# Loading the adaLN slabs from GpSimd's queue instead of SyncE's in a hybrid decoder layer

## The chip, the core and the metric

The kernel runs on one core of a Trainium2 chip. A core has TensorE (PE, with its weight loads PEld), VectorE (DVE), ScalarE (ACT), GpSimd (POOL) and SyncE (SP), and 16 DMA engines which every queue of the core uses. Each engine works through its own instructions strictly in order and waits where the next one's inputs are not ready. The metric is the device time of one execution in microseconds (us), lower is better.

## What is computed

One layer with sequence 256 and width 2048, all in float32. A vector c gives six modulation vectors (adaLN), x is normalised and modulated to h, h goes through one combined input projection into four mixers (differential attention, mLSTM, GLA, S5), their outputs are gated, summed and projected, and a SwiGLU feed-forward follows, again modulated.

```
mod = (silu(c) @ ada_w + ada_b).reshape(6, 2048)       # ada_w is 2048 x 12288: 96 slabs of 1 MB
shift_m, scale_m, gate_m, shift_f, scale_f, gate_f = mod
h = rms(x, g0) * (1 + scale_m) + shift_m
proj = h @ w_in                                        # 2048 x 5656: the projections of all four mixers
o_a, o_b, o_c, o_d = diff_attention, mlstm, gla, s5    # each 256 x 512
mix = sum_i sigmoid(h @ w_gate[i] + b_gate[i]) * (o_i @ w_branch[i])
x = x + gate_m * rms(mix @ w_out, g1)
h = rms(x, g2) * (1 + scale_f) + shift_f
a, g = split(h @ ffn_w_in)
x = x + gate_f * rms((silu(a) * g) @ ffn_w_out, g3)
```

## The kernel before

Every large weight comes in slabs of 128 x 2048 float32 (1 MB) through `load` (L114 to L122), one DMA each. A weight slab is split by `split` (L126) in two halves of 1024 columns: ACT rounds a half into `whi` (L137), DVE writes the rest `wlo = raw - whi` (L75), and TensorE multiplies with `mm3t` (three matmuls of 512 columns for each pair of k block and token block). The slab buffers `raw` are a ring of three (NR = 3). The split halves are a ring of four (NB = 4) and one more while the mixers run (NX = 1).

An adaLN slab is never multiplied on TensorE. `ada_tile` (L204 to L209) loads it, and one DVE instruction, a SCALAR_TENSOR_TENSOR at L83 over 128 x 2048, multiplies it with the broadcast silu(c) in `cb` and adds up each row into one column of `ada`. The first 32 slabs (shift_m and scale_m, vectors 0 and 1) make h. They use a ring of their own, `raw0`, of four buffers (NA = 4), whose first two hold the two token blocks `xt` of x until these have been normalised and transposed. All later slabs share the ring `raw` with the weights.

The input projection runs in four rounds of four k blocks (ROUNDS). In round 0, the first four of the eleven groups of 512 columns are multiplied in plain float32 from slabs of their own (`wlead`, eight halves of 512 KB) so that the matmuls of k block 0 can begin as soon as `xq` of k block 0 is ready: slabs 2k and 2k+1 give the shift and the scale of k block k, then L75 adds the bias, L83 makes `amul`, L80 scales `xq`, and L267 and L75 split it into `hx`. The other seven groups of round 0, and all groups of rounds 1 to 3, need `hx` of four k blocks and the split weights. While round r runs, the generator `chunks` makes the eight slabs of round r+1. 48 further slabs (vectors 2 to 4) are spread by `take_ada` over the gates, branches and output projection, and 16 (vector 5) over the feed-forward.

The kernel is written against a tile framework that orders the instructions of each engine itself, from the order of the code, priorities and an estimate of when each is ready. So moving a load to another queue also moves other instructions. Before, SP issues all loads in one order. Each queue may have up to eight DMAs under way: a ninth waits for one of the eight completion semaphores.

Of the kernel before, what the change touches and what calls it, by code (L numbers as in the profile page):

```python
# [69 lines left out]
def trunk(ctx: ExitStack, tc: tile.TileContext, A: dict, out: bass.AP):  # L70
    nc = tc.nc
    ve, se, te, sy = nc.vector, nc.scalar, nc.tensor, nc.sync
# [42 lines left out]
    def load(src, ada=False):  # L115
        if ada and early[0] is not None:
            raw = early[0].tile([P, 2048], F32, name="raw0", tag="raw0", bufs=NA)
        else:
            raw = ring.tile([P, 2048], F32, name="raw", tag="raw", bufs=NR)
        w = src.shape[-1]  # L120
        sy.dma_start(raw[:, :w], src)
        return raw[:, :w]  # L122

    wide, turn = [None], [0]
# [23 lines left out]
    def weights(src, pool=None, nb=NB, tag=None):  # L148
        return split(load(src), pool, nb, tag)
# [52 lines left out]
    ada = cp.tile([P, 96], F32, name="ada")  # L202

    def ada_tile(v, j):  # L204
        raw = load(A["ada"][v, j], ada=True)
        col = ada[:, v * 16 + j : v * 16 + j + 1]
        stt(raw, raw, 1.0, cb, MUL, MUL, accum=col)
        if v > 1 and j == 15:
            tt(ada[:, v * 16 : v * 16 + 16], ada[:, v * 16 : v * 16 + 16], vp[:, v * 16 : v * 16 + 16], ADD)  # L209
# [19 lines left out]
    for tok in range(2):  # L229
        for h in range(2):  # L230
            src, col = xt[tok][:, h * 1024 : h * 1024 + 1024], ssx[:, 2 * tok + h : 2 * tok + h + 1]
# [7 lines left out]
        for h in range(2):  # L239
            src = xt[tok][:, h * 1024 : h * 1024 + 1024]  # L240
# [460 lines left out]
    def mixer_s5():  # L701
# [54 lines left out]
        for n in range(4):  # L756
# [65 lines left out]
            act(z[:, n, :], z[:, n, :], AF.Gelu_apprx_tanh)  # L822
            yield
        gw = load(A["glu_w"])
        for n in range(4):
            pg = mxtile()
# [445 lines left out]
```

## Time and profile before

| | |
|---|---|
| time, median of three runs | 1661.66 us (1660.12 to 1664.41) |
| time of the profiled execution | 1662.55 us |
| its span, first to last instruction | 1660.8 us, granted TensorE clock 0.997 of full speed |
| busy PE, DVE, ACT, POOL | 1627.5, 1202.2, 827.9, 0.2 us |
| bytes moved by DMA | 400.60 MB, mean 241 GB/s |

A profile gives each engine's busy time, a timeline with what ended the idle time before an instruction, and for each queue when it issued a DMA. Matmuls are pipelined, so a busy PE is not a PE at its peak: the number of matmuls in a stretch tells more than its busy share. SPq is the issue of a DMA on SyncE's queue; the time beside it is that of issuing, not of the transfer.

### The profile page before, as it was taken

How to read it: one execution, taken by the hardware profiler on the slowest of the kernel's cores; microseconds unless marked ns; L12 is line 12 of the kernel's file. 1: busy time of each engine (PE TensorE's matmuls, PEld its weight loads, DVE VectorE, ACT ScalarE, POOL GpSimd, SP SyncE). 2: the span in 40 equal slices, each digit the busy share in tenths (PEclk: the TensorE clock that was granted, in tenths of full speed). 3: DMA queues.
4: the chain of work that ended last, by engine and by line, in shares of the span. 5: the costliest groups of instructions: out<-in, count | busy, mean ns of one | idle time of the engine just before them, and what ended most of it. 6: DMA issues, size and time to landing. Idle time of an engine off the chain costs nothing.

```text
span 1660.8 us, 19104 instructions
## 1 busy us (share of the span) xinstructions
PE 1627.5 (98%) x7376; PEld 1311.1 (79%) x7376; DVE 1202.2 (72%) x1611; ACT 827.9 (50%) x1108; POOL 0.2 (0%) x4
## 2 busy tenths in 40 slices
PE   8999999999999999999999999999999999999997
PEld 5677888777787777777888788888888888888886
DVE  6899999899899998997756755565656554544444
ACT  2443355678765465465446644444444444444442
POOL 0000000000000000000000000000000000000000
PEclk9999999999999999999999999999999999999999
DMA  9988887866557875775576266666666655655553
GB/s 369 376 339 310 327 330 283 295 250 224 197 212 257 297 260 203 258 274 204 179 256 249 104 218 236 247 234 243 239 242 229 224 192 190 216 192 188 202 186 118
DMA packets 61267, 400.60 MB, mean 241 GB/s; under 512 B 7023, under 2 KB 10612, under 8 KB 13816
## 3 DMA queue, kind: packets, MB, share of 16 engines
q1 hardware_dynamic: 60600, 398.33, 65.4%
q8 instruction: 58, 0.95, 0.2%
q10 hardware_dynamic: 576, 1.05, 0.2%
q14 instruction: 33, 0.27, 0.0%
HBM read 397.23 MB, written 2.12 MB: 240 GB/s over the span
## 4 chain that ended last, share of the span: by engine, by line
PE 83%; DVE 10%; ACT 3%; DMA 2%; issue 2%; DVEq 0%; SPq 0%; ACTq 0%
PE mmt L96 77%; PE mxt L96 3%; DVE wlo L75 3%; DMA raw<-in_ada 2%; DVE raw L83 2%; PE hs L96 1%; DVE pc L75 1%; DVE pc L807 1%; ACT whi L137 1%; DVE pq L75 1%; DVE xc L75 1%; ACT L93 1%; PE mxt L1087 1%; PE ys L96 1%; DMA xt<-in_x_tok 0%
## 5 line engine op out<-in xcount | busy, mean ns | idle before, releaser
L75 DVE TENSOR_TENSOR wlo<-raw,whi 128x1024 fp32r<-128x1024 f32 x540 | 653.3, 1219 | 388.6 <-ACT whi L137 373.0
L137 ACT CAST whi<-raw 128x1024 fp32r<-128x1024 f32 x540 | 563.1, 1051 | 655.9 <-PE mmt L96 473.0
L96 PE MATMUL mmt<-whi,hx 128*128 128x512 f32 x1568 | 501.3, 395 | 1.6 <-ACT whi L137 1.6
L96 PE MATMUL mmt<-whi,h 128*128 128x512 f32 x1408 | 438.2, 391 | 1.9 <-ACT h L1031 1.2
L96 PEld LDWEIGHTS mmt<-whi,hx 128*128 128x128 f32 x1568 | 295.0, 189 | 68.4 <-issue 6.0
L96 PE MATMUL mmt<-wlo,hx 128*128 128x512 f32 x784 | 309.4, 395 | 4.1 <-DVE wlo L75 4.1
L96 PEld LDWEIGHTS mmt<-whi,h 128*128 128x128 f32 x1408 | 264.1, 188 | 58.0 <-ACT h L1031 2.3
L96 PE MATMUL mmt<-wlo,h 128*128 128x512 f32 x704 | 274.1, 389 | 0.0
L83 DVE SCALAR_TENSOR_TENSOR raw<-raw,cb 128x2048 f32<-128x2048 f32 x96 | 219.4, 2287 | 7.7 <-DMA raw<-in_ada 7.1
L96 PE MATMUL mmt<-whi,hid 128*128 128x512 f32 x704 | 217.3, 389 | 0.0
L96 PEld LDWEIGHTS mmt<-wlo,hx 128*128 128x128 f32 x784 | 148.1, 189 | 38.0 <-DVE wlo L75 6.4
L96 PEld LDWEIGHTS mmt<-whi,hid 128*128 128x128 f32 x704 | 132.2, 188 | 27.6
L96 PEld LDWEIGHTS mmt<-wlo,h 128*128 128x128 f32 x704 | 132.2, 188 | 26.9
L96 PE MATMUL mmt<-wlo,hid 128*128 128x512 f32 x352 | 136.9, 389 | 0.0
L96 PE MATMUL mmt<-whi,os 128*128 128x512 f32 x256 | 83.3, 400 | 0.2
L96 PE MATMUL mmt<-whi,mx 128*128 128x512 f32 x256 | 79.2, 390 | 0.0
L96 PEld LDWEIGHTS mmt<-wlo,hid 128*128 128x128 f32 x352 | 66.1, 188 | 13.5
L93 ACT ACT_TABLE_LOAD x57 | 73.1, 1283 | 4.5 <-DVE fx L80 2.9
L96 PEld LDWEIGHTS mmt<-whi,os 128*128 128x128 f32 x256 | 47.8, 188 | 14.1 <-ACT whi L137 1.5
L96 PEld LDWEIGHTS mmt<-whi,mx 128*128 128x128 f32 x256 | 48.1, 188 | 9.8
L96 PE MATMUL mmt<-wlo,os 128*128 128x512 f32 x128 | 51.1, 401 | 3.1 <-DVE wlo L75 3.1
L96 PE MATMUL mmt<-wlo,mx 128*128 128x512 f32 x128 | 50.1, 391 | 0.0
(300 smaller groups left out, 1062.4 us busy)
## 6 DMA issues: line engine op xcount, KB each, us to landing
raw<-in_ada SPq DMA_DIRECT2D x96, 1024.0 KB, 5.2
raw<-in_ffn_in SPq DMA_DIRECT2D x88, 1024.0 KB, 5.1
raw<-in_w_gate SPq DMA_DIRECT2D x64, 1024.0 KB, 5.0
raw<-in_ffn_out SPq DMA_DIRECT2D x44, 1024.0 KB, 4.9
raw<-in_w_in SPq DMA_DIRECT2D x40, 1024.0 KB, 7.2
raw<-in_w_branch SPq DMA_DIRECT2D x16, 1024.0 KB, 5.0
raw<-in_w_out SPq DMA_DIRECT2D x16, 1024.0 KB, 4.9
wlead<-in_w_lead SPq DMA_DIRECT2D x8, 512.0 KB, 13.1
```

The lines of the kernel that those rows point to most:

```text
L75: return ve.tensor_tensor(out=o, in0=a, in1=b, op=op)
L83: return ve.scalar_tensor_tensor(out=o, in0=a, scalar=s, in1=b, op0=op0, op1=op1, accum_out=accum)
L93: return se.activation(out=o, in_=i, func=f, **kw)
L96: return te.matmul(o, lhsT=l, rhs=r, start=start, stop=stop, skip_group_check=True)
L137: se.copy(hi[:, :n], s)
L807: ve.tensor_tensor_scan(out=pc[:, c, :], data0=mg, data1=pc[:, c, :], initial=0.0, op0=MUL, op1=ADD)
L1087: te.transpose(ps[:, n * 256 + tok * P : n * 256 + tok * P + P], sa[tok][:, c : c + P], ident)
```

## The change

```
@@ -118,7 +118,7 @@
         else:
             raw = ring.tile([P, 2048], F32, name="raw", tag="raw", bufs=NR)
         w = src.shape[-1]
-        sy.dma_start(raw[:, :w], src)
+        (nc.gpsimd if ada else sy).dma_start(raw[:, :w], src)
         return raw[:, :w]
```

All 96 adaLN slabs are issued by GpSimd, which has nothing else to do after its first four memsets. Weights, x and everything else stay on SyncE, whose DMAs fall from 419 to 323. Buffers, arithmetic and the number of matmuls (7107) stay. ACT_TABLE_LOAD instructions on ACT go from 57 to 63, because the framework interleaves the mixers' activations differently.

On SP, at the start of the program, before (`xt` the token blocks, `raw0` adaLN slabs 0 to 3, `wlead` the lead weights in halves):

```order
L182 DMA xt_95<-in_x_tok 128x2048
L182 DMA xt_97<-in_x_tok 128x2048
L121 DMA raw0_237<-in_ada 128x2048
L121 DMA raw0_240<-in_ada 128x2048
L259 DMA vp_74<-in_vp 128x252
L345 DMA wlead_151<-in_w_lead 128x1024
L345 DMA wlead_152<-in_w_lead 128x1024
L121 DMA raw0_260<-in_ada 128x2048
L121 DMA raw0_263<-in_ada 128x2048
L345 DMA wlead_153<-in_w_lead 128x1024
L345 DMA wlead_154<-in_w_lead 128x1024
```

On SP at the same place after the change (`raw_332` and `raw_374` are the first two weight slabs of round 0):

```order
L182 DMA xt_95<-in_x_tok 128x2048
L182 DMA xt_97<-in_x_tok 128x2048
L259 DMA vp_74<-in_vp 128x252
L121 DMA raw_332<-in_w_in0 128x2048
L121 DMA raw_374<-in_w_in0 128x2048
L345 DMA wlead_151<-in_w_lead 128x1024
L345 DMA wlead_152<-in_w_lead 128x1024
L345 DMA wlead_153<-in_w_lead 128x1024
L345 DMA wlead_154<-in_w_lead 128x1024
L345 DMA wlead_155<-in_w_lead 128x1024
L345 DMA wlead_156<-in_w_lead 128x1024
L345 DMA wlead_157<-in_w_lead 128x1024
```

The adaLN slabs are gone from this queue, and two weight slabs of 1 MB have moved ahead of all lead weights. On POOL the slabs stand alone, in the order 0, 1, 2 and so on.

On DVE, around the scaling of k block 3, before (`raw0_304` and `raw0_307` are slabs 6 and 7, which give its scale and shift, `raw0_371` is slab 8, `hx_311` is h of k block 3, `wlo_335` and `wlo_339` are the two halves of the first weight slab of round 0):

```order
L83 SCALAR_TENSOR_TENSOR raw0_304,ada_148<-raw0_304,cb_73 128x2048
L83 SCALAR_TENSOR_TENSOR raw0_307,ada_148<-raw0_307,cb_73 128x2048
L75 TENSOR_TENSOR ada_148<-ada_148,vp_74 128x2
L83 SCALAR_TENSOR_TENSOR amul_225<-ada_148,vp_74 128x1
L80 TENSOR_SCALAR xq0_173<-xq0_173,amul_225,ada_148 128x256
L267 CAST hx_311<-xq0_173 128x256
L75 TENSOR_TENSOR hx_311<-xq0_173,hx_311 128x256
L75 TENSOR_TENSOR wlo_335<-raw_332,whi_334 128x1024
L75 TENSOR_TENSOR wlo_339<-raw_332,whi_338 128x1024
L83 SCALAR_TENSOR_TENSOR raw0_371,ada_148<-raw0_371,cb_73 128x2048
```

On DVE at the same place after the change, from behind slab 7 on (`raw0_413` is slab 9, `hx_289` is h of k block 2):

```order
L267 CAST hx_289<-xq0_173 128x256
L75 TENSOR_TENSOR ada_148<-ada_148,vp_74 128x2
L75 TENSOR_TENSOR wlo_381<-raw_374,whi_380 128x1024
L75 TENSOR_TENSOR hx_289<-xq0_173,hx_289 128x256
L83 SCALAR_TENSOR_TENSOR amul_225<-ada_148,vp_74 128x1
L83 SCALAR_TENSOR_TENSOR raw0_371,ada_148<-raw0_371,cb_73 128x2048
L80 TENSOR_SCALAR xq0_173<-xq0_173,amul_225,ada_148 128x256
L83 SCALAR_TENSOR_TENSOR raw0_413,ada_148<-raw0_413,cb_73 128x2048
L267 CAST hx_311<-xq0_173 128x256
L75 TENSOR_TENSOR ada_148<-ada_148,vp_74 128x2
L75 TENSOR_TENSOR wlo_425<-raw_422,whi_424 128x1024
L75 TENSOR_TENSOR hx_311<-xq0_173,hx_311 128x256
```

The scaling of `xq` for k block 3 now stands behind slab 8, and the finished `hx` of k block 3 behind slab 9 and five weight halves; for k blocks 0 to 2 it is the same by two slabs each.

## Rows read from the trace of the kernel before

**Rows 1.** Page, part 1: busy us (share of the span) xinstructions
```profile
PE 1627.5 (98%) x7376; PEld 1311.1 (79%) x7376; DVE 1202.2 (72%) x1611; ACT 827.9 (50%) x1108; POOL 0.2 (0%) x4
```

**Rows 2.** Windows: stretch, its length, busy (xinstructions) by engine, PEclk, DMA share, GB/s
```profile
0.00:50.00 50.00, 40.15 (x127) 23.60 (x128) 33.92 (x56) 15.04 (x26) 0.20 (x4) 1.00 0.95 378
50.00:100.00 50.00, 46.68 (x194) 36.20 (x193) 42.10 (x54) 25.28 (x34) 0.00 (x0) 0.97 0.86 347
100.00:150.00 50.00, 50.00 (x222) 41.23 (x221) 48.18 (x63) 20.69 (x23) 0.00 (x0) 1.00 0.86 325
...
1000.00:1050.00 50.00, 50.00 (x226) 41.53 (x225) 28.88 (x26) 21.25 (x23) 0.00 (x0) 1.00 0.65 236
```

**Rows 3.** Windows of 10 us, same columns, while the queue is never empty
```profile
20.00:30.00 10.00, 10.00 (x23) 4.33 (x24) 7.32 (x12) 0.00 (x0) 0.00 (x0) 1.00 1.00 403
...
40.00:50.00 10.00, 8.31 (x20) 3.41 (x20) 7.03 (x10) 3.17 (x4) 0.00 (x0) 1.00 1.03 425
```

**Rows 4.** Timeline of DVE, start: start us, us, instruction [idle before <-releaser]
```profile
6.83 1.23 DVE L83 SCALAR_TENSOR_TENSOR sq<-xt 128x1024 f32<-128x1024 f32 x1 [3.05 <-DMA xt<-in_x_tok]
...
19.45 0.41 DVE L80 TENSOR_SCALAR xq<-xq,amul,ada 128x256 f32<-128x256 f32 x1
...
21.37 2.29 DVE L83 SCALAR_TENSOR_TENSOR raw<-raw,cb 128x2048 f32<-128x2048 f32 x1 [0.72 <-DMA raw<-in_ada]
...
40.63 2.29 DVE L83 SCALAR_TENSOR_TENSOR raw<-raw,cb 128x2048 f32<-128x2048 f32 x1 [1.52 <-DMA raw<-in_ada]
```

**Rows 5.** Timeline of SP: issue of slabs 2 and 3, and of 6 and 7
```profile
14.61 0.96 SPq L121 DMA_DIRECT2D raw<-in_ada  x2
...
23.70 2.76 SPq L121 DMA_DIRECT2D raw<-in_ada  x2
```

**Rows 6.** Timeline of PE: lead of k blocks 0, 1 and 3, first split group, its last small group
```profile
19.97 1.96 PE L96 MATMUL mxt<-wlead,xq 128*128 128x512 f32 x4 [1.84 <-issue]
...
27.00 1.98 PE L96 MATMUL mxt<-wlead,xq 128*128 128x512 f32 x4
...
43.83 1.98 PE L96 MATMUL mxt<-wlead,xq 128*128 128x512 f32 x4 [1.69 <-DVE xq L80]
...
50.40 0.79 PE L96 MATMUL mmt<-whi,hx 128*128 128x512 f32 x1
...
281.24 0.28 PE L96 MATMUL mmt<-hx,wlo 128*128 128x256 f32 x1
```

**Rows 7.** Chain of work that ended last: start us, us, what
```profile
102.41 5.44 PE hs L96 x24
```

**Rows 8.** Timeline of DVE, back to back: what one slab and one half cost
```profile
63.02 2.29 DVE L83 SCALAR_TENSOR_TENSOR raw<-raw,cb 128x2048 f32<-128x2048 f32 x1
...
65.23 2.29 DVE L83 SCALAR_TENSOR_TENSOR raw<-raw,cb 128x2048 f32<-128x2048 f32 x1
...
69.07 4.63 DVE L75 TENSOR_TENSOR wlo<-raw,whi 128x1024 fp32r<-128x1024 f32 x4
73.61 2.29 DVE L83 SCALAR_TENSOR_TENSOR raw<-raw,cb 128x2048 f32<-128x2048 f32 x1
...
118.95 0.69 DVE L75 TENSOR_TENSOR da_k<-mmt,da_k 128x512 f32<-128x512 f32 x1
119.55 2.28 DVE L83 SCALAR_TENSOR_TENSOR raw<-raw,cb 128x2048 f32<-128x2048 f32 x1
```

**Rows 9.** Page, part 6: queue and kind xcount, KB each, us to landing
```profile
out_x<-x SPq DMA_DIRECT2D x4, 256.0 KB, 2.4
out_x<-x ACTq DMA_DIRECT2D x4, 256.0 KB, 2.6
```

**Rows 10.** Waits, 300 to 950 us: engine <- releaser: us in total, times, longest
```profile
ACT whi L137 <- DMA raw<-in_w_branch: 41.0, 11, 6.5
```

**Rows 11.** Timeline of DVE: two of its faster instructions at the start
```profile
10.08 1.42 DVE L79 TENSOR_SCALAR xt<-xt,ssx 128x1024 f32<-128x1024 f32 x2
```

**Rows 12.** Page, part 5: table loads of ACT
```profile
L93 ACT ACT_TABLE_LOAD x57 | 73.1, 1283 | 4.5 <-DVE fx L80 2.9
```

More of the change, by code (lines that the diff above doesn't have):

```diff
@@ L120, in load @@
         w = src.shape[-1]
-        sy.dma_start(raw[:, :w], src)
+        (nc.gpsimd if ada else sy).dma_start(raw[:, :w], src)
         return raw[:, :w]
```

## The prediction

> **What bounds the kernel now.** I read the page's busy shares first, then windows of equal length, then the timelines of the first 110 us. TensorE is busy 98% of the span [rows 1]. Counted in matmuls, a stretch of the feed-forward is full: 226 in 50 us [rows 2]. From 100 us on the projection rounds run at 222 in 50 us, and DVE is almost as full there, 48.18 of 50 us [rows 2]: two engines share the limit. Only the first 100 us lie well below, with 127 and 194 matmuls, and the DMA engines are busy 0.95 of the first 50 us [rows 2]. So the change, which touches no matmul, can win or lose at the start, where data is late, and hardly elsewhere.
>
> The start is a chain over adaLN slabs: DVE scales `xq` of k block 0 at 19.45, PE begins its lead at 19.97, and at k block 3 DVE waits 1.52 us for slab 7 until 40.63 and PE begins at 43.83, having waited 1.69 us for `xq` [rows 4, 6]. The first group with split weights starts at 50.40 [rows 6]. What a delay of that moment costs depends on what PE loses later. From 50.40 to the last small group of the projection at 281.24 [rows 6] there stand 973 matmuls of 512 columns and 12 of 256. A group of 24 takes 5.44 us [rows 7], 0.2267 each, and a half one about 0.12, so 222.0 us of work: it could end at 272.4. **PE loses 8.8 us there**, mostly before 100 us.
>
> **Removed and added.** SP's queue loses 96 issues. It issued slabs 2 and 3 together in 0.96 us [rows 5]: that time is hidden, since the transfers behind are far longer (a 1 MB slab at the 403 to 425 GB/s of a queue that never runs dry [rows 3] takes 2.5 us). What goes is the waiting of weights behind slabs: `load` of a weight can now pass a slab whose buffer isn't free. POOL gains 96 issues and has no other work [rows 1]. What one costs on POOL no row shows: at best the 0.48 us of an issue on SP [rows 5], at worst, as an estimate, a landing time of a small DMA more, 2.4 us [rows 9]. I take the lower one, since the issue runs ahead of the data except at slab 2; the upper one adds 2 us to the start.
>
> **The start, moved.** Two queues now have work at once. How the engines divide themselves no row shows at this size; the nearest is the end of the program, where four DMAs of SP and four of ACT land after 2.4 and 2.6 us [rows 9], so I take equal shares: 5.05 us a slab. The token blocks and slabs 0 and 1 now travel together, 4.2 MB in 10.1 us from about 2.3, so the first token block lands near 9.3, 2.5 us after the 6.83 of before [rows 4]. Slab 2 takes over its buffer, and its issue, at 14.61 before [rows 5], moves by the same to 17.1. It lands at 17.1 + 5.05 + 2.4 (landing [rows 9]) = 24.6, slabs 3 to 7 every 5.05 us, to 49.8. Meanwhile SP brings x, two weight slabs, the lead weights and two more weight slabs, 10 MB. Then its queue is blocked, as the three `raw` buffers wait for splits that stand behind slabs in DVE's order. So slab 8 comes at full rate, by 52.5, and slab 9 by 55.
>
> DVE's new order makes it later. The scaling of `xq` of k block 0 stands behind slab 2 now: 24.6 + 2.21 (a slab on DVE [rows 8]) + 0.45 = 27.3 instead of 19.45. That of k block 3 stands behind slab 8, which DVE reaches at 54.0 after slab 7 and a weight half: 54.0 + 2.21 + 0.45 = 56.7. The leads of k blocks 0 to 2 take 7.0 us each (19.97 to 27.00 [rows 6]) and are hidden under the 10 us between two k blocks. From k block 3's lead to the first split group it takes 6.6 us as before [rows 6], so **63.3 instead of 50.40: 12.9 us later.** `hx` of k block 3 is ready before that, at 60.9.
>
> **What comes back.** With PE starting later, most weights of round 0 are split by then (five halves), so the 8.8 us of stalls have no reason left but DVE. From slab 8 to the half that PE needs in the third group of round 2, DVE has 25 slabs of 2.21, 42 halves of 1.14 ((73.61 - 69.07) / 4), 20 additions of 0.60 [rows 8] and some 21 us of small instructions: 136.6 us, done at 190.6. PE needs it after 543 matmuls of 512 columns and 8 of 256, 124.1 us, at 187.4. That is the largest lag that I find in the four rounds: 3.2 us. Before round 1, where 12 slabs stand ahead (20 of 32 against 16 before), DVE is still 2 us early. So **12.9 - 8.8 + 3.2 = 7.3 us later** at the end of the projection.
>
> **The mixers, 300 to 950 us.** Slabs and weights share three buffers on either queue, so their slots come free in the same order. ACT waits 41.0 us for branch weights [rows 10], some of it for a weight that queues behind a slab; side by side a weight can land sooner by up to 2.5 us and a slab later by as much. The six more table loads cost ACT 6 x 1.28 = 7.7 us [rows 12], while it is busy half the time [rows 1]. I put 0 on PE for all of it, bounds -2 and +6. In the feed-forward PE is full and DVE idles 21 of 50 us [rows 2], which hides 16 slabs: 0.
>
> Sum: the profiled execution took 1662.55 us, its span 1660.8; 1662.55 + 7.3 = 1670. The median of the runs is 0.9 us lower: **1669 us.**
>
> **Rivals.**
> - *Slabs come first* (faster). If POOL's queue gets what it asks for, k block 3 is bound by bytes: nine slabs and 8.5 MB of SP's queue, 17.9 MB in 43 us, so 47.0 with start and landing, and the split groups start at 53.6, 3.2 us late. DVE is then ahead and the stalls go: 3.2 - 8.8 = -5.6, 1656. It decides from a POOL share of about two thirds. For it: the slabs no longer queue behind lead weights. Against it: DVE's order puts a slab more before each k block whatever the shares.
> - *No measurable difference.* If SP's queue is served first, its 10 MB end at 27, then slabs land every 2.5 us and DVE's 7.1 us for each pair sets the pace: k block 3 at 53.5, groups at 60.1, and 9.7 - 8.8 + 3 = +4: 1666. Or the order of transfers matters less than I think and only the issuing is saved: 96 x 0.48 = 46 us on SP [rows 5], all hidden: 1662. The Trainium skill states that second way as a rule (DMA: Bandwidth & Descriptors, Issuing engines are not separate DMA queues): DMAs of all engines interleave on the same DMA engines, and issuing from several only saves the time of issuing. I give it little, since the slabs stand ahead of other work on DVE now, which this rule doesn't speak of.
> - *Slabs starve.* The Trainium skill (SBUF — State Buffer, SBUF: two separate sides) says that GpSimd writes the descriptors of its DMAs through a port that VectorE takes for itself in some fast instructions, casts and scalings, and the DMA waits for them. It speaks against this change. As a mechanism here: TENSOR_SCALAR runs at 0.71 us for 1024 columns [rows 11] against 1.14 for a weight half [rows 8], so it is one of the fast ones, but such instructions are few. If instead any DVE instruction held a slab's issue, ten slabs of the start would each wait about one of 1.2 to 2.2 us: 12 to 22 us more, 1681 to 1691.
> - *The mixers pay.* Late slabs hold DVE, which is in order, and PE behind it: the upper bound of 6 us, and half of the old stalls (4.4) staying: 1679.
>
> **How the numbers follow.** About 0.3%, 5 us, is what a measurement of this kernel can tell from no change: 1656.7 to 1666.6. I give the forecast (1664 to 1677) 0.6, slabs first 0.12, no difference 0.16, the last two 0.12 together. The range 1659 to 1677 leaves out most of the first and the last two. Slower: most of 0.6 and 0.12, 0.63. Same: 0.16 and the low end of the forecast, 0.27. Faster: 0.10.
>
> **What would show it.** After the change: the first token block near 9.3, `xq` of k block 0 near 27, lead of k block 3 near 57, first split group near 63, last small group of the projection near 289; slabs landing 5 us apart while SP's queue is full; and a feed-forward as long as before. A first split group before 55 refutes the shares; one at 63 with an end of the projection at 281 refutes the lag of DVE; a longer stretch from 300 to 950 points to the mixers.

## The result, and the profile after the change

The changed kernel takes 1682.11 us (median of 4 runs, 1679.85 to 1685.28) against 1661.88 us of the kernel before (4 runs): a ratio of 1.0118, 95% interval 1.0102 to 1.0135. It is slower, as forecast, but by 20 us instead of 7, and lies outside the range. The profiled execution took 1684.29 us, 21.7 more than that of before.

First the page, parts 1, 5 and 6, in lines that answer to [rows 1] and [rows 12] (part 5: busy us, mean ns of one | idle us before them and what ended it):

```profile
PE 1633.3 (97%) x7376; PEld 1314.1 (78%) x7376; DVE 1197.5 (71%) x1611; ACT 834.7 (50%) x1114; POOL 51.1 (3%) x100
...
L83 DVE SCALAR_TENSOR_TENSOR raw<-raw,cb 128x2048 f32<-128x2048 f32 x96 | 219.7, 2288 | 29.5 <-DMA raw<-in_ada 29.0
...
L93 ACT ACT_TABLE_LOAD x63 | 80.8, 1283 | 8.4 <-DVE mlkc L83 3.8
...
raw<-in_ada POOLq DMA_DIRECT2D x96, 1024.0 KB, 5.4
```

DVE idles 29.5 us in front of the 96 slabs, nearly all of it until a slab lands. The same group of before is

```profile
L83 DVE SCALAR_TENSOR_TENSOR raw<-raw,cb 128x2048 f32<-128x2048 f32 x96 | 219.4, 2287 | 7.7 <-DMA raw<-in_ada 7.1 <-ACT cb L199 0.3
```

The windows that answer to [rows 2] (same columns):

```profile
0.00:50.00 50.00, 33.87 (x106) 21.98 (x107) 30.26 (x48) 16.73 (x27) 6.14 (x15) 0.97 0.96 391
50.00:100.00 50.00, 47.51 (x182) 34.41 (x181) 46.20 (x67) 19.57 (x27) 6.86 (x13) 0.97 0.99 396
100.00:150.00 50.00, 47.38 (x205) 37.39 (x204) 45.60 (x62) 21.19 (x27) 3.17 (x6) 1.00 0.86 335
1000.00:1050.00 50.00, 50.00 (x227) 41.51 (x226) 28.88 (x26) 21.19 (x23) 1.06 (x2) 1.00 0.62 228
```

PE runs 106, 182 and 205 matmuls where it ran 127, 194 and 222; the feed-forward is as full as before. The DVE, POOL and PE timelines of the start answer to [rows 4 to 6]:

```profile
10.48 1.23 DVE L83 SCALAR_TENSOR_TENSOR sq<-xt 128x1024 f32<-128x1024 f32 x1 [6.79 <-DMA xt<-in_x_tok]
...
29.15 0.41 DVE L80 TENSOR_SCALAR xq<-xq,amul,ada 128x256 f32<-128x256 f32 x1
30.64 2.29 DVE L83 SCALAR_TENSOR_TENSOR raw<-raw,cb 128x2048 f32<-128x2048 f32 x1 [1.08 <-DMA raw<-in_ada]
...
52.92 2.29 DVE L83 SCALAR_TENSOR_TENSOR raw<-raw,cb 128x2048 f32<-128x2048 f32 x1 [0.84 <-DMA raw<-in_ada]
55.14 0.41 DVE L80 TENSOR_SCALAR xq<-xq,amul,ada 128x256 f32<-128x256 f32 x1
```

```profile
18.54 0.53 POOL L121 DMA_DIRECT2D raw<-in_ada  x1 [16.11 <-PE mxt L247]
```

```profile
29.66 3.53 PE L96 MATMUL mxt<-wlead,xq 128*128 128x512 f32 x4 [3.43 <-issue]
...
55.61 2.70 PE L96 MATMUL mxt<-wlead,xq 128*128 128x512 f32 x4 [2.49 <-DVE xq L80]
...
63.87 0.79 PE L96 MATMUL mmt<-whi,hx 128*128 128x512 f32 x1
...
291.78 0.28 PE L96 MATMUL mmt<-hx,wlo 128*128 128x256 f32 x1
```

The first split group starts at 63.87 instead of 50.40 and the last small group of the projection at 291.78 instead of 281.24. To follow the loss further I use the **lag**: each matmul's start in one trace less the start of the same matmul in the trace of before (the nth of the same line, tiles and shape), as the median over all matmuls that before started in a stretch. It is 13.5 us at 50 to 75 us, 10.5 at 250 to 275, 20.1 at 475 to 500, 21.7 at 1000 to 1050, and stays there. So **half is lost by the end of the projection, and half in the mixers, between 280 and 500 us.** In the rows one matmul shows it, the first of `ys`, 17.5 us late (before, then after):

```profile
454.64 0.63 PE L96 MATMUL ys<-xc,cd 128*32 128x256 f32 x4 [0.94 <-DVE xc L75]
```

```profile
472.11 0.63 PE L96 MATMUL ys<-xc,cd 128*32 128x256 f32 x4 [2.22 <-DVE xc L75]
```

Behind that wait of 2.22 us the granted clock fell (the number after the five engines); in the trace of before it stood at 1.00 from 452 to 470 us:

```profile
473.00:477.00 4.00, 4.00 (x22) 2.76 (x22) 2.48 (x6) 2.75 (x3) 0.53 (x1) 0.57 0.41 109
```

4 us at 0.57 are some 1.7 us lost, as an estimate, so that much of the mixers' part is the clock.

From the last small group on, the same 199 us of before take 208. Windows of that stretch, before and after (busy us of PE, PEld, DVE, ACT, POOL):

```profile
281.24:480.00 198.76, 196.95 (x1016) 155.35 (x1015) 178.43 (x337) 151.21 (x259) 0.00 (x0) 1.00 0.65 237
```

```profile
291.78:500.00 208.22, 199.19 (x1013) 155.16 (x1012) 171.31 (x294) 147.58 (x249) 8.54 (x16) 0.99 0.63 223
```

DVE does 7 us less work there and idles 37 us instead of 20. The waits from 300 to 500 us (total, times, longest) name the new idle time, first before, then after:

```profile
DVE raw L83 <- DMA raw<-in_ada: 1.6, 2, 1.5
```

```profile
DVE raw L83 <- DMA raw<-in_ada: 15.8, 8, 4.5
```

One of these waits, on POOL and DVE:

```profile
313.39 0.53 POOL L121 DMA_DIRECT2D raw<-in_ada  x1 [10.24 <-DVE raw L83]
```

```profile
310.80 2.29 DVE L83 SCALAR_TENSOR_TENSOR raw<-raw,cb 128x2048 f32<-128x2048 f32 x1 [2.77 <-DMA raw<-in_ada]
...
313.02 1.22 DVE L75 TENSOR_TENSOR wlo<-raw,whi 128x1024 fp32r<-128x1024 f32 x1
318.77 2.29 DVE L83 SCALAR_TENSOR_TENSOR raw<-raw,cb 128x2048 f32<-128x2048 f32 x1 [4.54 <-DMA raw<-in_ada]
```

One slab frees its buffer at 313.0, POOL issues the next into it at 313.39, and in DVE's order a single weight half (1.22 us) stands between the two. The load takes 5.4 us, so DVE stands still for 4.54.

### The profile page after: what moved, and what is told of

It is laid out like the page before. It is cut to its first block, busy times and chain, and to the rows that moved or that the text cites. A ratio compares the mean times of both kernels' runs of the same rounds, so it can differ in the third digit from the quotient of the medians.

```text
span 1682.5 us, 19215 instructions
## 1 busy us (share of the span) xinstructions
PE 1633.3 (97%) x7376; PEld 1314.1 (78%) x7376; DVE 1197.5 (71%) x1611; ACT 834.7 (50%) x1114; POOL 51.1 (3%) x100
## 3 DMA queue, kind: packets, MB, share of 16 engines
q10 hardware_dynamic: 576, 1.05, 0.2%
## 4 chain that ended last, share of the span: by engine, by line
PE 63%; DVE 14%; issue 11%; DMA 9%; ACT 3%; POOL 0%; SPq 0%; DVEq 0%; POOLq 0%; ACTq 0%
PE mmt L96 60%; DVE wlo L75 5%; DMA raw<-in_ada 3%; DVE raw L83 2%; DMA raw<-in_w_in 2%; DMA raw<-in_w_gate 1%; PE mxt L96 1%; ACT whi L137 1%; DMA raw<-in_w_branch 1%; DVE pc L75 1%; DVE pq L75 1%; DVE xc L75 1%; DVE pc L807 1%; PE mxt L1087 1%; DMA xt<-in_x_tok 1%
## 5 line engine op out<-in xcount | busy, mean ns | idle before, releaser
L83 DVE SCALAR_TENSOR_TENSOR raw<-raw,cb 128x2048 f32<-128x2048 f32 x96 | 219.7, 2288 | 29.5 <-DMA raw<-in_ada 29.0
L96 PEld LDWEIGHTS mmt<-whi,hid 128*128 128x128 f32 x704 | 132.2, 188 | 27.3
L121 POOL DMA_DIRECT2D raw<-in_ada x96 | 50.9, 530 | 1269.4 <-DVE wlo L75 823.0
```

Of the source, the lines that this page charges most:

```text
L83: return ve.scalar_tensor_tensor(out=o, in0=a, scalar=s, in1=b, op0=op0, op1=op1, accum_out=accum)
L96: return te.matmul(o, lhsT=l, rhs=r, start=start, stop=stop, skip_group_check=True)
L121: (nc.gpsimd if ada else sy).dma_start(raw[:, :w], src)
```

## The experiments

Two theories stood at the start. **The queue costs**: a slab on GpSimd's queue comes later. **The order costs**: the framework, which estimated other times, put DVE's instructions into an order that waits. To take them apart I held DVE, ACT and PE to a given list (issue order alone, no wait is added):

```
+def keep_order(tc):
...
+    how = mybir.DependencyInfo(mybir.DependencyClass.NoSync, mybir.DependencyReason.DATA)
+    for steps in json.loads(zlib.decompress(base64.b85decode(ORDER))).values():
...
+            if prev is not None:
+                tc.add_manual_dep(here[name], prev, how, reason="order")
...
     with tile.TileContext(nc) as tc:
         trunk(tc, aps, out)
+        keep_order(tc)
```

That the hold itself costs nothing measurable is seen in late_pool_oldorder (1662.71). Held are DVE, ACT and PE; the order in which SyncE issues its DMAs is still the framework's. What was measured, all in one table (ratio: to runs of the kernel before beside it, medians 1661.43 to 1663.16; lag as above; wait: DVE for slabs from 300 to 500 us, in us):

```
kernel                  median us  ratio [95%]              lag at 50  250   475   1000  wait
after                   1682.11    1.0118 [1.0102, 1.0135]    13.5    10.5  20.1  21.7  15.8
pool_oldorder           1672.05    1.0058 [1.0042, 1.0075]     7.0     7.3   7.7   9.8   2.4
sp_neworder             1699.19    1.0222 [1.0203, 1.0240]    23.2    25.1  33.7  36.2  16.0
early_pool              1674.45    1.0070 [1.0048, 1.0091]    11.9     7.8   9.4  11.5   2.4
late_pool               1675.67    1.0084 [1.0065, 1.0102]    -1.5    -1.5   7.4  11.4  11.7
pool_after8             1669.38    1.0043 [1.0028, 1.0058]     6.5     5.3   5.4   5.7   2.1
late_pool_oldorder      1662.71    1.0005 [0.9996, 1.0014]    -1.4    -1.2  -0.7   1.4   2.7
pool_olddve             1669.13    1.0042 [1.0027, 1.0057]     7.2     0.9   4.8   6.8   3.7
pool_smallslabs         1673.22    1.0062 [1.0045, 1.0079]    13.2    10.2  10.8  13.1   1.8
before_smallslabs       1661.38    0.9991 [0.9981, 1.0000]    -1.8    -3.2  -3.1   0.7   0.0
pool_neworder_oldslabs  1722.17    1.0363 [1.0347, 1.0378]    11.6     7.8  34.7  58.9   6.1
pool_oldorder_newslabs  1728.56    1.0403 [1.0386, 1.0419]     6.8     7.2  40.8  65.7  27.4
pool_laterslabs         1713.54    1.0315 [1.0297, 1.0333]    10.5    10.0  42.6  49.6   9.3
pool_newdve_olds5       1688.59    1.0151 [1.0131, 1.0171]    12.9     8.8  26.2  31.2  19.4
```

### Queue and order exchanged

The new queue with the old order (pool_oldorder): `keep_order` with the lists of the kernel before.

> The changed kernel (slabs on GpSimd's queue), but DVE, ACT and PE are held to the order of instructions that they had before the change; only the queues differ from the kernel before. Theory A (the order costs): the changed kernel loses most of its 20 us because its DVE order puts slabs ahead of weight halves and right behind the release of their own buffer. Then with the old order only the sharing of the DMA engines in the first 50 us stays, some 4 us at the end: 1664 to 1668, waits of DVE for slabs back from 29 us to under 15. Theory B (the queue costs): a slab on GpSimd's queue is issued or lands later whatever the order; then this kernel is as slow as the changed one, 1678 to 1685, and DVE's waits for slabs stay near 29 us or grow.

The old queue with the new order (sp_neworder): the kernel before, with the lists of the changed kernel.

> The kernel before (all slabs on SyncE's queue), but DVE, ACT and PE are held to the order of instructions that they have after the change; the other half of the exchange. Theory A (the order costs): 1675 to 1685, with DVE waiting 20 us or more for slabs. Theory B (the queue costs): 1660 to 1665, as the kernel before.

Measured: 1672.05 and 1699.19. Waits from 300 to 500 us, first pool_oldorder, then sp_neworder:

```profile
DVE raw L83 <- DMA raw<-in_ada: 2.4, 2, 1.8
```

```profile
DVE raw L83 <- DMA raw<-in_ada: 16.0, 8, 3.8
```

The waits of the mixers follow the order, whichever queue brings the slabs, and with them the lag: from 250 to 475 us it grows by 0.4 us with the old order and by 8.6 with the new one on SyncE's queue. In the mixers the order is nearly all. But the start is the queue's: with the old order the lag is 7.0 us at 50, where I had expected 4 to remain, and all of it stays. Of these, 3.4 arise at the first token block, which starts on DVE at 10.27 instead of 6.83 [rows 4], as it now shares the engines with slabs 0 and 1. The rest comes up to k block 1, and it is not only the second queue's: in pool_oldorder too SyncE issues two weight slabs at 3.07 and 3.77 us, ahead of the lead weights, where before the first came at 29.28. How much of the rest is that order, no run tells. So theory A was right on the mixers and too cheap on the start. And the new order is one that only the new queue can bear: on SyncE's queue it costs 36 us, 23 of them by 50 us, with the granted clock at 0.50 from 25 to 48 us.

### The two halves of the change

Only the first 40 slabs on GpSimd's queue (early_pool), and only the other 56 (late_pool):

```
-        (nc.gpsimd if ada else sy).dma_start(raw[:, :w], src)
+        (nc.gpsimd if ada and early[0] is not None else sy).dma_start(raw[:, :w], src)
```

```
-        (nc.gpsimd if ada else sy).dma_start(raw[:, :w], src)
+        (nc.gpsimd if ada and early[0] is None else sy).dma_start(raw[:, :w], src)
```

> Only the first 40 slabs (all that make h, and 8 more up to the end of the projection) go over GpSimd's queue, the later 56 over SyncE's as before. In the changed kernel the matmuls of the end of the projection stand 10.5 us later than before and those of 500 us some 20 us. If the two losses are separate: the projection ends 10 to 11 us late and nothing is added after it, 1671 to 1674. If a late start makes the mixers late by itself: 1680 or more. If the loss of the projection is made up later: 1662 to 1666.

> Only the later 56 slabs go over GpSimd's queue, the first 40 over SyncE's as before. If the two losses are separate, the projection ends at 281 us as before and 9 to 11 us are lost between 280 and 500 us: 1671 to 1674. If the late start caused the loss in the mixers: 1660 to 1665.

Measured: 1674.45 and 1675.67, each a little above the range expected and somewhat more than half the loss. late_pool ends the projection 1.5 us early and then loses 8.9 us by 500 us, so a late start is not what makes the mixers slow. early_pool ends it 7.8 us late and loses 1.6 more by 500 us, with 2.4 us of waits. It has 63 table loads of ACT as the changed kernel has, so these six are not the price either.

### The start

All slabs but the first eight on GpSimd's queue, with the old order (pool_after8):

```
+        nslab[0] += ada
-        (nc.gpsimd if ada else sy).dma_start(raw[:, :w], src)
+        (nc.gpsimd if ada and nslab[0] > 8 else sy).dma_start(raw[:, :w], src)
```

> As the kernel with GpSimd's queue and the old order of DVE, ACT and PE, but the first eight slabs (k blocks 0 to 3 of h) are loaded on SyncE's queue as before the change; the other 88 stay on GpSimd's. With the old order and all slabs on GpSimd, PE's matmuls stood 7.1 us later from 45 us on, and hardly more from there to 850 us. Theory C (the start is lost to the sharing of the DMA engines by two queues while h of the first k blocks is awaited): the 7.1 us go, matmuls stand within 1 us of before, and the time is 1660 to 1666. Rival (GpSimd's queue is slow for each slab, wherever it stands): slabs 8 to 31 are late as well, at least half of the 7.1 us stays, 1667 to 1672.

Measured: 1669.38, a number that fits the rival, but the rows tell of theory C at another place. The lead of k blocks 0 to 2 is back (19.86, 27.57 and 35.20 against 19.97, 27.00 and 35.00). Then GpSimd's queue begins with slab 8, and k block 3 is 2.6 us late, not for a slab, but for its lead weights on SyncE's queue, where SyncE's order up to them is that of before. POOL, then PE:

```profile
32.11 0.66 POOL L123 DMA_DIRECT2D raw<-in_ada  x1 [31.66 <-DVE raw L83]
```

```profile
46.43 3.75 PE L96 MATMUL mxt<-wlead,xq 128*128 128x512 f32 x4 [4.10 <-DMA wlead<-in_w_lead]
```

In that wait the clock fell, and k block 3's lead and the gap behind it took 10.71 us (46.43 to 57.14) where they took 6.57, so that more of the lag of 6.5 us is the clock than the late weights:

```profile
45.00:52.00 7.00, 5.57 (x7) 2.50 (x8) 1.41 (x5) 0.00 (x0) 0.53 (x1) 0.52 1.02 424
```

So what was awaited when the second queue began came later; that moment moved, and most of the loss remained. With the first 40 slabs on SyncE's queue and the old order held (late_pool_oldorder, the edit of late_pool with `keep_order`), neither of the two causes is left:

> The later 56 slabs on GpSimd's queue, the first 40 on SyncE's, and DVE, ACT and PE held to their order of before the change. If the queue costs only where two queues have work at once at the start, and the mixers lose only by the order, nothing is left to lose: matmuls within 1.5 us of before all along, DVE's wait for the 16 slabs of the mixers under 4 us, 1660 to 1666. If GpSimd's queue costs something for each slab after all (a slab lands 0.3 to 0.4 us later there): 1668 or more, as some 40 slabs stand in the part that is not full.

Measured: 1662.71, ratio 1.0005. A slab on GpSimd's queue by itself costs nothing that can be measured, though it lands a little later (median from 300 to 500 us: 5.3 us in the changed kernel, 5.0 before). It is also no gain: of the kernels here that load every slab whole none beats the one before.

### The mixers: is it the wait for the slabs' data?

The changed kernel with its order held and the last 56 slabs cut to 64 columns (pool_smallslabs), and the same cut in the kernel before (before_smallslabs, with `sy`). Both leave out most of these slabs' data, and DVE multiplies `cb` by itself in its place:

```
+        if ada and early[0] is None:
+            nc.gpsimd.dma_start(raw[:, :64], src[:, :64])
+            return raw
...
-        stt(raw, raw, 1.0, cb, MUL, MUL, accum=col)
+        stt(raw, raw if early[0] is not None else cb, 1.0, cb, MUL, MUL, accum=col)
```

> The changed kernel with its own order of DVE, ACT and PE held, but the last 56 slabs (mixers and feed-forward) are loaded only by their first 64 columns (32 KB instead of 1 MB), and DVE multiplies cb by itself there: a transfer is left out, the instruction and its wait for the DMA stay. Theory D (the mixers' loss of 10 us is DVE waiting for slabs that are issued only when their buffer comes free): the wait for each shrinks by the time of the transfer, DVE's waits for slabs between 290 and 500 us fall from 15.9 to under 5 us, and the lag of PE's matmuls behind those of before grows from 10.5 by less than 5 us there instead of by 9.6: 1674 to 1678. Rival E (other instructions that stand elsewhere, S5's parameters and six more table loads): the lag still grows by 8 to 10 us, 1680 to 1684.

> The control to the changed kernel with small slabs: the kernel before (SyncE's queue, its own order held), with the last 56 slabs loaded only by their first 64 columns and DVE multiplying cb by itself there; 55 MB of transfers are left out, all instructions and waits stay. Theory D (in the new order the mixers lose by waiting for slabs): the old order waits only 1.6 us for slabs there, so the matmuls of 500 us stand at most 3 us earlier than before, 1657 to 1663. Rival G (the transfers left out speed up the weights whatever the order, so the small slabs proved nothing): matmuls at 500 us at least 6 us earlier, 1650 to 1656.

Measured: 1673.22 and 1661.38. With the transfers cut, the new order's lag goes from 10.2 to 10.8 between 250 and 475 us, where it went from 10.5 to 20.1, and the waits fall to 1.8 us. The old order gains nothing from the same cut there (-3.2 and -3.1; these 3 us arise before 100 us, where the program is the same as that of before). So the mixers' loss is the new order waiting for the slabs' loads; the bandwidth that these 56 loads take is worth nothing to the old order.

Holding DVE alone to its old list, with ACT and PE ordered anew (pool_olddve: `keep_order` with one list):

> The changed kernel with DVE alone held to its old order; ACT and PE are ordered anew by the framework. If DVE's order carries the loss of the mixers, it is as fast as with all three held: the lag of PE at the end of the projection is 7 to 8 us and grows by less than 3 us to 500 us, 1670 to 1674. If ACT's order (more table loads) or PE's carries it: it grows by 6 us or more, 1676 to 1684.

Measured: 1669.13, below both expectations, by another split. The lag falls from 7.2 to 0.9 us in the first 250 us and grows by 3.9 to 475 us, 1.7 of these at 390 us, where the clock fell (0.58 from 390 to 394). PE's waits explain much of the first: in 50 us from the first split group on, pool_oldorder has those of before, pool_olddve has none of them. pool_oldorder, 57 to 107 us:

```profile
PE mmt L96 <- ACT whi L137: 1.6, 1, 1.6
PE mmt L96 <- DVE wlo L75: 1.4, 3, 0.8
```

With the old stalls went a fall of the clock: 0.62 from 69 to 73 us before, 1.00 from 70 to 80 in pool_olddve. So the stalled time of PE does come back, as I had forecast, but only when ACT and PE are ordered anew. Which of the two lists does it was not tested.

### Which instructions make the order wait

Four kernels move single instructions on DVE. New order with the last 56 slabs at their old places (pool_neworder_oldslabs), and the reverse (pool_oldorder_newslabs); a place is the weight half behind which a slab stands. The list of the former changes as here, against the changed kernel:

```
-L83 SCALAR_TENSOR_TENSOR raw_2476,ada_148<-raw_2476,cb_73 128x2048
 L75 TENSOR_TENSOR wlo_2411<-raw_2408,whi_2410 128x1024
-L83 SCALAR_TENSOR_TENSOR raw_2551,ada_148<-raw_2551,cb_73 128x2048
 L83 SCALAR_TENSOR_TENSOR lg_2286<-mxt_2289,biasT_2096 128x128
...
 L75 TENSOR_TENSOR wlo_2415<-raw_2408,whi_2414 128x1024
+L83 SCALAR_TENSOR_TENSOR raw_2476,ada_148<-raw_2476,cb_73 128x2048
```

> The changed kernel with its own order of ACT and PE held, and of DVE too, but each of the last 56 slabs is put behind the weight half behind which it stood before the change; seven of the first 13 move up to three halves later, the rest hardly. Theory D1 (these places of the slabs make the waits): the lag of PE grows by less than 4 us between 290 and 500 us, 1672 to 1678. Rival E (the other instructions that the new order moves): the lag still grows by 8 to 10 us, 1680 to 1684.

> The other half of the exchange: GpSimd's queue and the old order of DVE, ACT and PE, but each of the last 56 slabs is put on DVE behind the weight half behind which it stands after the change. Theory D1: the lag of PE, 7.3 us at the end of the projection, grows by 6 to 10 us in the mixers, 1678 to 1683. Rival E: it grows by less than 3 us, 1671 to 1675.

Measured: 1722.17 and 1728.56. Neither theory said that. The exchange was not clean: it put every slab directly behind its half, ahead of the small instructions of the mixers that had stood between them. Then each of the 16 first slabs some 3 us later in the new order (pool_laterslabs):

```
-L83 SCALAR_TENSOR_TENSOR raw_2551,ada_148<-raw_2551,cb_73 128x2048
 L83 SCALAR_TENSOR_TENSOR lg_2286<-mxt_2289,biasT_2096 128x128
...
 L75 TENSOR_TENSOR wlo_2415<-raw_2408,whi_2414 128x1024
+L83 SCALAR_TENSOR_TENSOR raw_2551,ada_148<-raw_2551,cb_73 128x2048
```

> The changed kernel with its own order, except that on DVE each of the 16 first slabs from the shared buffers (290 to 520 us) stands some 3 us of other instructions (3 to 9 of them) later. Theory D (DVE reaches these slabs before they land): the idle time before the 16 falls from 18.1 us to under 7, and the lag of PE's matmuls grows from 290 to 500 us by less than 6 us instead of 9.6: 1674 to 1679. Rival F (a slab that is used later holds its buffer longer, so the next load through the same three buffers is later and the wait only moves): the idle time moves to weight halves and the lag grows by 9 us or more, 1681 to 1690.

Measured: 1713.54, rival F and much more of it. DVE waits less for slabs (9.3 instead of 15.8 us), but ACT waits more for the weights that go through the same three buffers (3.8 us in the changed kernel, 9.4 before, 300 to 500 us):

```profile
ACT whi L137 <- DMA raw<-in_w_gate: 16.6, 6, 6.1
...
DVE raw L83 <- DMA raw<-in_ada: 9.3, 3, 3.9
```

The three buffers are a loop: a load can start only when a use has ended, so time given to a slab is taken from a weight. That is argued, and these waits are too short for the 32.6 us by which the lag grows from 250 to 475 us. The slabs now also stand behind small instructions that wait themselves: DVE waits 8.1 us for PE in front of `lg` (1.6 before), and PE 8.3 us for `lg` (0.8 in the changed kernel). What each of the two costs was not taken apart. Last, 48 small instructions of S5's parameters, which the new order runs in round 3 and the old one in the mixers, put back alone (pool_newdve_olds5):

```
-L75 TENSOR_TENSOR sp_2231<-vp_74 128x16
 L75 TENSOR_TENSOR wlo_1752<-raw_1745,whi_1751 128x1024
-L75 TENSOR_TENSOR sp_2231<-sp_2231,vp_74 128x16 x2
...
```

> The changed kernel with DVE held to its new order except for the 48 small instructions that prepare S5's parameters: these go back behind the same number of weight halves as before the change (out of round 3, into the mixers). ACT and PE are ordered by the framework, as in the changed kernel. Theory H (DVE reaches the slabs of the mixers before they land because these instructions no longer stand between them): DVE's waits for slabs from 300 to 500 us fall from 15.8 to under 7 us, and the lag of PE's matmuls grows there by less than 5 us instead of 9.6: 1673 to 1678. Rival I (the places of slabs and weight halves themselves make the waits): 12 us of waits or more stay, and the lag grows by 8 us or more, 1680 to 1690.

Measured: 1688.59, 19.4 us of waits; theory H falls. That they had left the stretch (the 7 us less of DVE's work) is not what makes DVE early.

How long DVE waits for slabs, though not the time of a kernel, roughly follows from a sum that can be made from a list alone. For each of the 16 first slabs of the shared buffers I added up the DVE work that stands between the last use of its buffer and the slab (2.21 us a slab, 1.14 a half [rows 8], the small ones by their columns), and how far that falls short of 5.3 us, the landing of a slab. It is an estimate from lists and rows, beside the idle time measured in front of these 16:

```
kernel             short of 5.3 us, sum (slabs short)   idle measured
before                    4.5  (3)                           1.6
early_pool                9.3  (7)                           3.7
pool_laterslabs          11.0  (5)                           9.3
late_pool                12.2  (7)                          11.8
pool_newdve_olds5        17.5  (7)                          22.1
sp_neworder              20.8 (11)                          16.0
after                    20.8 (11)                          18.1
```

In the new list 11 of 16 loads have less than 5.3 us of work to hide behind, in the old one 3. The two exchanged kernels fit as well: a like count gives some 9 us for pool_neworder_oldslabs and 24 for pool_oldorder_newslabs, and they idle 6.1 and 29.6 us. But their lags grow by 26.9 and 33.6 us from 250 to 475 us, and that of pool_laterslabs by 32.6: a small sum does not make a fast list. That the sum is the cause of the idle time is argued, from kernels that it ranks only roughly; no run changed it and left all else in place.

## Why the prediction was wrong

**The start: right in its steps, with some luck in the sum.** Token block 10.48 (forecast 9.3), issue of slab 2 at 18.54 (17.1), `xq` of k block 0 at 29.15 (27.3), lead of k block 3 at 55.61 (56.7), first split group at 63.87 (63.3). Slabs 3 to 8 start on DVE from 30.64 to 52.92, 4.5 us apart (5.05). The first steps came 1.2 to 1.9 us late, the slabs made that good, and the clock added 1.7 us to k block 3's lead (8.26 us instead of 6.6): the errors cancelled to 0.6 us. The equal shares were the assumption on which it hung, and they hold roughly. The trace by queue, 20 to 30, 30 to 40 and 40 to 50 us (packets, MB, share of the 16 engines), GpSimd's first:

```profile
q0 software_dynamic: 286, 2.12, 50.7%
q1 hardware_dynamic: 559, 2.04, 50.6%
...
q0 software_dynamic: 385, 2.85, 68.9%
q1 hardware_dynamic: 376, 1.35, 33.1%
...
q0 software_dynamic: 301, 2.20, 53.5%
q1 hardware_dynamic: 306, 1.95, 47.0%
```

In bytes the shares are equal in the first and nearly so in the third; in the second GpSimd's queue moved twice as much, in as many packets, as its packets were twice as large. The Trainium skill states (DMA: Bandwidth & Descriptors, Queues, rings and completion order) that each DMA engine takes the queues that have work in turn, packet by packet. By that rule, as far as it is the packets of these rows, their numbers would be equal: the second and third stretches agree, the first, with 286 and 559, does not.

**What comes back: the sign right, place and size off.** I took 8.8 us of old stalls as gone and 3.2 us of new lag of DVE in round 2. The lag of the matmuls falls from 13.5 to 7.0 us by 105 us, so 6.5 came back; then it rises by 4.6 in round 1, where I had DVE 2 us early, and ends at 10.5 instead of 7.3. The clock in the lead of k block 3 (below) may be part of these 3.2 us: early_pool, without that fall, ends the projection 7.8 us late. pool_oldorder and pool_olddve show that the stalled time returns by the new order of ACT and PE, not by the later start.

**The step that failed is the one on the mixers:** "I put 0 on PE for all of it, bounds -2 and +6". They took 9.6 us to 500 us and 11.2 in all (some 1.7 of it the clock). The premise, that slots come free in the same order on either queue, said nothing on how much work stands between a slot's release and its next use, and that is what changed: 1.6 us of waits became 15.8. I had looked there at what the move of a load could do (2.5 us sooner or later) and at six table loads, and not at DVE's list, which the framework had reordered there too. The rival "the mixers pay" named the mechanism, late slabs that hold DVE and PE behind it, but its price was taken from the bound of 6 us, and its chance was small.

**The other rivals.** "Slabs first" asked for two thirds of the engines; GpSimd's queue moved 7.17 of 12.51 MB from 20 to 50 us, 57%. "No difference" is what late_pool_oldorder shows, 1.0005, for the 56 slabs behind the start; at the start, with the same order of the engines, the move cost 7.0 us, since it changes which bytes come first. The Trainium skill states as a rule that issuing from several engines saves only the time of issuing (DMA: Bandwidth & Descriptors, Issuing engines are not separate DMA queues); the first number agrees with it, the second does not. "Slabs starve" came to 1681 to 1691, and the time lies there, but not by that way: an issue on POOL takes 0.53 us, a slab lands after 5.4 us instead of 5.2 (page, part 6), and the same waits stand in sp_neworder without GpSimd's queue. The feed-forward is unchanged, as forecast.

## What to carry to other kernels

Where a framework orders the instructions, a change of queue is a change of order, and the two must be priced apart: hold the order, and the queue shows its own price. For each load through a shared ring, count the work that stands between the last use of its buffer and its own use, and compare that with the time of its landing: it tells where the engine will wait, and not what another list would cost, as pool_laterslabs shows. Here the second queue was neutral where no load of the first was waited for (late_pool_oldorder), and took half to two thirds of the bytes while something was.

## What the hardware showed that was not expected

The granted clock falls to 0.50 (1.2 of 2.4 GHz) for short stretches at different moments of otherwise equal programs, and these decide one or two microseconds each. In the changed kernel it fell while the lead of k block 3 ran, after PE had waited 2.49 us for `xq`; that lead took 8.26 us (55.61 to 63.87) against 6.57 before. Windows, the clock is the number after the five engines:

```profile
57.00:60.00 3.00, 3.00 (x5) 1.21 (x4) 3.00 (x6) 0.00 (x0) 0.53 (x1) 0.50 1.00 415
```

It need not follow: in pool_oldorder it fell behind a wait of 1.06 us at the start of the feed-forward's `h`, and in the profile of before, behind the same wait of 1.05 us, it stayed at 1.00. Both rows, pool_oldorder first:

```profile
931.00:933.00 2.00, 2.00 (x8) 1.68 (x7) 2.00 (x7) 1.89 (x8) 0.00 (x0) 0.50 0.89 250
```

```profile
920.00:923.00 3.00, 2.48 (x11) 1.55 (x12) 3.00 (x9) 1.90 (x7) 0.00 (x0) 1.00 0.28 68
```

before_smallslabs, the same program as before up to the last 56 slabs, stands 3.2 us ahead of it at 250 us. So the lags of single traces in the table hold to about 3 us, and the times of several runs are what the verdicts rest on. None of the four lists that I made by hand was as fast as the framework's two. The other surprise is the size of what a list can cost: moving 16 slabs by 3 to 9 small instructions on an engine that idles 18% of the stretch cost 31 us more.
